# Part of the adaLN projection moved from TensorE to VectorE, and caches loaded earlier, in a two-layer diffusion backbone step

## Chip, cores and metric

One core of a Trainium2 chip runs the whole program in one launch. The metric is device time in microseconds (us). The kernel before took 1877.81 us as the median of three runs (1877.62, 1877.81 and 1882.55). A core has five engines that run their own instruction streams: PE (TensorE, matrix products), DVE (VectorE), ACT (ScalarE), POOL (GpSimd) and SP (SyncE, which here issues the DMAs). Each takes its instructions in program order and waits on semaphores for the others.

## The reference

Two layers work on 128 prompt tokens and 512 sample tokens of width 1024, in fp32. Each layer does, for either token group with its own conditioning vector:

```python
sh1, sc1, g1, sh2, sc2, g2 = split(silu(cond) @ ada_w[l] + ada_b[l], 6)   # adaLN, 1024 -> 6*1024
mix = mixers((x * (1 + sc1) + sh1) @ w_in[l])   # differential attention | neighbourhood attention | mLSTM
x = layer_norm(ALPHA * x + g1 * (mix @ w_out[l]))
y = square(relu((x * (1 + sc2) + sh2) @ w_mlp1[l])) @ w_mlp2[l]           # 1024 -> 4096 -> 1024
x = layer_norm(ALPHA * x + g2 * y)
```

There are two conditioning vectors (prompt and sample), so adaLN is a product of a 2 x 1024 matrix with a 1024 x 6144 matrix in each layer. The differential and the neighbourhood attention of the sample tokens also attend to 256 cached keys; the neighbourhood one adds a bias from a table per head.

## The kernel before

**Numbers.** Every fp32 matrix is split into a high and a low fp32r part; a product is three matmuls, high by high, high by low, low by high (`mul3`, L98 to L100), or two where one side is stacked (`mul2`, L106). A weight piece is split by ACT, which makes the high part (L170), and DVE, which subtracts it for the low part (L117).

**Weights.** All weights come as raw tiles of 1 MB. `run` walks a plan of units, finds the order in which the units first use each weight, and issues the loads in that order on SP (L208) into a ring of two buffers (`raw`). A buffer is free again when its four pieces are split into a slot, or, for an adaLN tile, when the unit that uses it is through. The slots are wt0 and wt1, and in the MLP a third one in the region AK. A scheduler then fixes each engine's instruction order, and this order is what runs.

**adaLN.** The 1024 x 6144 matrix of a layer is cut into 24 chunks of 1024 x 256, six vectors (shift, scale, gate, twice) of four chunks each, 48 in all. `ada_units` does a chunk with eight fp32 matmuls into four groups of 32 partitions (L368) and a copy by ACT (L371). A later "pick" adds the groups: with two small products into columns (L385) and a bias add on DVE (L388) for a shift or a scale, or, for a gate (vectors 2 and 5), with one product into a row of two partitions (L380), a bias row loaded from DRAM (L379) and a store of the gate row. In the plan, layer 0's vectors 0 and 1 come at the start, 2 to 4 are woven into its attention, vector 5 and layer 1's 0 and 1 stand in the first MLP, layer 1's 2 to 4 in its attention, and its vector 5 in the second MLP.

**MLP.** The hidden width 4096 is worked in eight rounds. The ups of a round are eight units of 24 matmuls with 128 hidden rows and 384 or 256 token columns; relu squared is made by ACT and DVE (L1389, L1390), and its split by ACT (L1401) and DVE (L117). The downs of the round before are five units, one for each tile of 128 tokens, of 24 matmuls with 512 columns into a PSUM tile `ss`, of which there are two. The first round's downs are copied to Y by ACT (L1414), the later ones added to Y by DVE (L1416). `downs[c - 1]` stands behind `ups[c]` in the plan, with spare adaLN units woven in.

**Neighbourhood attention.** `prep` loads the queries and keys of a head (hq, hk), then the head's cached keys into ckf, one buffer (L891), splits them into the last 256 columns of hk (ACT L892, DVE L893), and loads the bias table rw (L896), from which POOL makes three masked tables bm (L901). The scores of a head against its own and its cached keys are `mul2` products of hk with hq. In the differential attention the cached keys come through cak, one buffer (L1007).

Of the kernel before, what the change touches and what calls it, by code (L numbers as in the profile page):

```python
# [42 lines left out]
PACK = (("abT", (DEPTH, 48)), ("lnT", (DEPTH, 4, KT)), ("ident", (P,)), ("sel2", (2,)), ("selr", (32,)),  # L43
# [25 lines left out]
class Step:  # L69
# [61 lines left out]
    def w_src(self, k):  # L131
        kind, l, j = k
        d = self.d
        if kind == "ada":
            return d["ada"][l, j]
# [43 lines left out]
    def run(self, plan):  # L179
# [32 lines left out]
        def try_split(slack=0):  # L212
            while state["split"] < state["dma"] and order[state["split"]][0] == "ada":
                state["split"] += 1
# [23 lines left out]
        for i, u in enumerate(plan):  # L238
# [3 lines left out]
            for k in u.w:  # L242
# [6 lines left out]
                if k[0] != "ada":  # L249
# [12 lines left out]
            for k in u.w:  # L262
                if k[0] == "ada" and last[k] == i:
                    del self.raw[k]
# [21 lines left out]
    def setup(self):  # L286
# [30 lines left out]
        nc.vector.tensor_tensor(self.condS, self.condS, e, ALU.mult)  # L317

# [39 lines left out]
    def ada_units(self, l, vecs, own=None):  # L358
# [15 lines left out]
        def pick(v, q, part):  # L374
            po = self.mm("pick")
            if v in (2, 5):
                ab = self.adp.tile([2, CW], F32, name="abrow", bufs=1)
                off = v * D + q * CW
                nc.sync.dma_start(ab, self.d["ada_b"][l, off:off + CW].partition_broadcast(2))  # L379
                nc.tensor.matmul(po[:32, :CW], self.selr, part, start=True, stop=True)  # L380
                nc.vector.tensor_tensor(ab, po[:2, :CW], ab, ALU.add)
                nc.sync.dma_start(self.s_gate[l][v // 3][:, q * CW:(q + 1) * CW], ab)
            else:
                for b in range(2):
                    nc.tensor.matmul(po[:, 2 * b:2 * b + 2], part[:, b * P:(b + 1) * P], self.sel2,  # L385
                                     start=True, stop=True)
                c0 = v * KT + 2 * q
                nc.vector.tensor_tensor(  # L388
                    self.adaF[l][:, v, 2 * q:2 * q + 2, :], po[:, :4].rearrange("p (a b) -> p a b", b=2),
                    self.abT[:, l, c0:c0 + 2, None].to_broadcast([P, 2, 2]), ALU.add)  # L390
# [4 lines left out]
        return out  # L395

# [173 lines left out]
    def head_load(self, l, kind, h):  # L570
# [4 lines left out]
        k = self.hp.tile([P, NTOK + PAST], F32R, name="hk", tag="hk", bufs=2)  # L575
        for g in range(2):
            o = slice(64 * g, 64 * g + 64)
            nc.sync.dma_start(q[o].bitcast(F32), self.s_q[kind + "q"][l][f][rows])
            nc.sync.dma_start(k[o, :NTOK].bitcast(F32), self.s_q[kind + "k"][l][f][rows, g])
# [274 lines left out]
    def b_proj(self, l):  # L854
# [16 lines left out]
        return u  # L871

    def b_attn(self, l):
# [14 lines left out]
        def prep(h):  # L888
            q, k = self.head_load(l, "b", h)
            ck = self.bw.tile([P, PAST], F32, name="ckf", tag="ckf", bufs=1)  # L890
            nc.sync.dma_start(ck, d["cbk"][l, :, h])  # L891
            nc.scalar.activation(k[:, NTOK:], ck, AF.Copy, scale=0.125)  # L892
            nc.vector.scalar_tensor_tensor(k[64:, NTOK:], ck[64:], 0.125, k[64:, NTOK:].bitcast(F32),  # L893
                                           op0=ALU.mult, op1=ALU.subtract)
            rw = self.bw.tile([P, 8, 48], F32, name="rw", tag="rw", bufs=1)
            nc.sync.dma_start(rw, d["rpbw"][l, h])  # L896
            bm = []
            for v in range(3):
                b = self.bw.tile([P, 8, 32], F32, name="bm", tag="bm", bufs=4)
                o = 16 + BLK_OFF[v]  # L900
                nc.gpsimd.tensor_tensor(b, rw[:, :, o:o + 32], self.nmask[:, v, None, :].to_broadcast([P, 8, 32]), ALU.add)  # L901
                bm.append(b)
            hold[h] = (q, k, bm)
            hold[h, "r"] = self.bw.tile([P, 5], F32, name="br", tag="br", bufs=2)

        def scores(h, c):
# [9 lines left out]
            else:  # L916
# [3 lines left out]
                kl = k[:, P:NTOK].rearrange("p (r w) -> p r w", r=8)[:, :, w]  # L920
                self.mul2(ps[:, :256], kl, qq, stack_stationary=False)
                self.mul2(ps[:, 256:], k[:, NTOK:], qq, stack_stationary=False)
# [64 lines left out]
    def a_proj(self, l):  # L987
        nc, d = self.nc, self.d

        def op():  # L990
# [9 lines left out]
            nc.sync.dma_start(self.AV[:, 0:2], d["cav"][l])  # L1000

        held = {}

        def cached(g):
            if g < 4:
# [485 lines left out]
    def layer(self, l):  # L1491
# [75 lines left out]
        if more:  # L1567
            spare += self.ada_units(l + 1, (0, 1)) + [self.mod_unit(l + 1, 0)]
# [155 lines left out]
```

## Time and profile before

| | us |
|---|---|
| median of three runs | 1877.81 |
| the profiled execution | 1881.12 |
| its span, first to last instruction | 1879.3 |
| PE busy | 1790.4 (95%) |
| DVE busy | 1083.5 (58%) |
| ACT busy | 724.3 (39%) |
| first MLP's rounds | about 498 to 940 |
| layer 1's attention around the moved adaLN chunks | about 1095 to 1290 |

A profile is one execution. An engine's busy time is summed over its instructions, with overlaps counted once; matmul records overlap each other, since the next starts before the last has ended. A wait is read from the bracket of a row: the idle time before the instruction and what it ended with. [...]

### The profile page before, as it was taken

What the parts mean: (1) busy time and instruction counts of PE and PEld (TensorE: products, weight loads), DVE (VectorE), ACT (ScalarE), POOL (GpSimd) and SP (SyncE); (2) the same over time, 40 slices, a digit from 0 to 9 for tenths busy, and PEclk for the clock granted to TensorE, in tenths of its full rate; (3) what the DMA queues carried; (4) which work ended last, traced back from release to release, by engine and by line L of the source; (5) the groups of instructions that cost most, each with busy time, mean ns of one, the idle gap of its engine ahead of it and who ended that gap; (6) DMA issues with size and microseconds to landing.
All of it is one profiled execution on the core that took longest, in us unless ns stands there. A gap on an engine that the chain in (4) does not pass through costs nothing.

```text
span 1879.3 us, 29111 instructions
## 1 busy us (share of the span) xinstructions
PE 1790.4 (95%) x11666; PEld 1607.1 (86%) x11666; DVE 1083.5 (58%) x2068; ACT 724.3 (39%) x1640; POOL 100.4 (5%) x153
## 2 busy tenths in 40 slices
PE   6999999998999999999999989988989999999996
PEld 4999888887888888888899988877879889998895
DVE  4755566787623343345777645677977134544477
ACT  3343235456533231232364423353566223322220
POOL 1111100000000000000010210000010000000001
PEclk9999999999999999999999989989999999999998
DMA  9555465321423332333336655461214224222221
GB/s 352 163 165 163 164 201 189 111 85 57 146 68 102 123 115 91 109 107 140 106 116 222 162 167 179 145 214 64 85 45 146 90 90 157 69 90 68 75 94 56
DMA packets 82712, 239.23 MB, mean 127 GB/s; under 512 B 31808, under 2 KB 44544, under 8 KB 63888
## 3 DMA queue, kind: packets, MB, share of 16 engines
q1 hardware_dynamic: 82576, 237.36, 38.2%
q8 instruction: 92, 1.51, 0.3%
q14 instruction: 44, 0.36, 0.1%
HBM read 210.78 MB, written 26.55 MB: 126 GB/s over the span
## 4 chain that ended last, share of the span: by engine, by line
PE 82%; DVE 9%; DMA 5%; ACT 2%; issue 1%; SPq 1%; POOL 0%; DVEq 0%; ACTq 0%
PE m L98 15%; PE m L99 15%; PE m L100 15%; PE ss L98 7%; PE ss L99 7%; PE ss L100 7%; PE ss L1115 1%; PE m L1145 1%; PE m L961 1%; PE m L368 1%; DVE wt L117 1%; DMA ada<-ada 1%; DVE anm L1118 1%; DMA z<-s_x 1%; PE mz L106 1%
## 5 line engine op out<-in xcount | busy, mean ns | idle before, releaser
L98 PE MATMUL m<-wt,Th 128*128 128x256 f32 (+2 forms) x864 | 274.8, 319 | 7.1 <-DVE Tl L1206 2.8
L99 PE MATMUL m<-wt,Th 128*128 128x256 f32 (+2 forms) x864 | 269.1, 312 | 0.0
L100 PE MATMUL m<-wt,Tl 128*128 128x256 f32 (+2 forms) x864 | 267.0, 311 | 0.0
L98 PE MATMUL m<-Th,AK 128*128 128x384 f32 (+1 forms) x736 | 229.3, 312 | 4.9 <-DVE Th L112 4.2
L99 PE MATMUL m<-Tl,AK 128*128 128x384 f32 (+1 forms) x736 | 229.1, 312 | 0.9 <-DVE Tl L117 0.9
L100 PE MATMUL m<-Th,AK 128*128 128x384 f32 (+1 forms) x736 | 225.9, 311 | 0.0
L170 ACT ACTIVATE wt<-raw 128x512 fp32r<-128x512 f32 x244 | 146.7, 627 | 149.3 <-PE ss L100 85.6
L117 DVE TENSOR_TENSOR wt<-raw,wt 128x512 fp32r<-128x512 f32 x244 | 162.3, 693 | 47.1 <-ACT wt L170 46.2
L98 PEld LDWEIGHTS m<-wt,Th 128*128 128x128 f32 x864 | 168.6, 195 | 22.4 <-issue 5.5
L100 PEld LDWEIGHTS m<-wt,Tl 128*128 128x128 f32 x864 | 167.4, 195 | 10.8 <-issue 3.1
L99 PEld LDWEIGHTS m<-wt,Th 128*128 128x128 f32 x864 | 169.0, 196 | 7.6 <-issue 1.7
L98 PE MATMUL m<-Th,wt 128*128 128x384 f32 (+1 forms) x536 | 166.4, 311 | 0.0
L100 PE MATMUL m<-Th,wt 128*128 128x384 f32 (+1 forms) x536 | 166.2, 310 | 0.0
L99 PE MATMUL m<-Tl,wt 128*128 128x384 f32 (+1 forms) x536 | 165.9, 310 | 0.0
L1416 DVE TENSOR_TENSOR Y<-ss,Y 128x1024 f32<-128x1024 f32 x60 | 73.2, 1223 | 156.8 <-PE ss L100 156.8
L1390 DVE SCALAR_TENSOR_TENSOR rl<-m,rl 128x384 f32<-128x384 f32 (+1 forms) x128 | 62.2, 488 | 164.5 <-ACT rl L1389 164.5
L98 PEld LDWEIGHTS m<-Th,AK 128*128 128x128 f32 x736 | 140.7, 191 | 8.8 <-DVE Th L112 4.7
L99 PEld LDWEIGHTS m<-Tl,AK 128*128 128x128 f32 x736 | 140.7, 191 | 3.7 <-issue 1.6
L100 PEld LDWEIGHTS m<-Th,AK 128*128 128x128 f32 x736 | 140.5, 191 | 1.0 <-issue 0.8
L98 PE MATMUL ss<-wt,hid 128*128 128x512 f32 x356 | 139.7, 395 | 0.0
L1389 ACT ACTIVATE rl<-m 128x384 f32<-128x384 f32 (+1 forms) x128 | 55.3, 434 | 218.8 <-PE m L100 216.1
L99 PE MATMUL ss<-wt,hid 128*128 128x512 f32 x356 | 138.8, 391 | 0.0
(705 smaller groups left out, 3554.4 us busy)
## 6 DMA issues: line engine op xcount, KB each, us to landing
raw<-w SPq DMA_DIRECT2D x64, 1024.0 KB
raw<-ada SPq DMA_DIRECT2D x40, 1024.0 KB
raw<-w_in SPq DMA_DIRECT2D x24, 1024.0 KB
ada<-ada SPq DMA_DIRECT2D x8, 1024.0 KB
raw<-w_out SPq DMA_DIRECT2D x8, 1024.0 KB
s_x<-Y SPq DMA_DIRECT2D x15, 512.0 KB
hq<-s_cq SPq DMA_DIRECT2D x16, 320.0 KB
nb<-s_nm SPq DMA_DIRECT2D x16, 320.0 KB
```

The source lines that it names most:

```text
L98: mt(out, a[0], b[0], start=first, stop=False)
L99: mt(out, a[0], b[1], start=False, stop=False)
L100: mt(out, a[1], b[0], start=False, stop=last)
L106: self.nc.tensor.matmul(out, a, b, start=first and i == 0, stop=last and i == 1)
L117: self.nc.vector.tensor_tensor(out, x, hi.bitcast(F32), ALU.subtract)
L170: self.nc.scalar.activation(hi, r, AF.Copy)
L368: nc.tensor.matmul(ps[32 * g:32 * g + 32, :CW], self.condS[:, kt, :], raw[:, kt, :], start=kt % 2 == 0, stop=kt % 2 == 1)
L961: nc.tensor.matmul(out[64 * i:64 * i + 64], w, rhs, start=b == 0, stop=b == nb - 1)
L1115: nc.tensor.matmul(ps[:, b, :384], qq[i], K[:, j, b * 384:b * 384 + 384], start=i == 0, stop=i == 1)
L1389: nc.scalar.activation(r[:, :n], ps[:, :n], AF.Relu)
L1390: nc.vector.scalar_tensor_tensor(r[:, :n], ps[:, :n], 0.0, r[:, :n], op0=ALU.max, op1=ALU.mult)
L1416: nc.vector.tensor_tensor(y, ps, y, ALU.add)
```

## The change

Of the 48 adaLN chunks 20 stay on TensorE: layer 0's vectors 0 to 4. The other 28 (layer 0's vector 5 and all of layer 1's) are done on VectorE in the first MLP. Their weights arrive transposed (`adaT`: 256 output rows of 1024 inputs in a 1 MB tile, two rows for each partition), and both conditioning vectors stand broadcast on all partitions (`condB`). A chunk is four multiply-and-sum operations over 128 x 1024, two output rows by two vectors; each sum lands in the column of `adaF` where it belongs. The bias add follows once for a vector. Gates are now kept as columns like the others, and `gate_rows` turns them into DRAM rows with two transposes, a copy and a DMA. In the plan one such chunk stands behind each down until there are none left: 5, 5, 4, 5, 5 and 4 in rounds 1 to 6, the unit that uses layer 1's first two vectors having one of the places.

The second part is the neighbourhood attention: the cached keys of all heads are loaded and split once a layer, before the projections of its queries, into a tile `BK` of their own; the first two bias tables are loaded there too, with two buffers, and the masked tables get six. The third is the cached keys of the differential attention: two buffers, and the first two loads are issued where the tiles are made.

```diff
+    def ada_dve(self, l, vecs):
+        nc = self.nc
+        def emit(v, q):
+            raw = self.raw[("adt", l, 4 * v + q)].rearrange("p (a b) -> p a b", b=D)
+            for b in range(2):
+                for j in range(2):
+                    x = self.mw.tile([P, D], F32, name="adx", tag="z2", bufs=2)
+                    nc.vector.scalar_tensor_tensor(x, raw[:, b], 1.0, self.condB[:, j], op0=ALU.mult, op1=ALU.mult,
+                                                   accum_out=self.adaF[l][:, v, 2 * q + b, j:j + 1])
+            if q == 3:
+                a = self.adaF[l][:, v]
+                nc.vector.tensor_tensor(a, a, self.abT[:, l, KT * v:KT * v + KT, None].to_broadcast([P, KT, 2]), ALU.add)
+                if v in (2, 5):
+                    self.gate_rows(l, v)
+        return [Unit(0, lambda v=v, q=q: emit(v, q), (("adt", l, 4 * v + q),), soft=True) for v in vecs for q in range(4)]
+    def gate_rows(self, l, v):
+        def rows():
+            pt = self.mm("pick")
+            for j in range(2):
+                nc.tensor.transpose(pt[:KT, j * P:j * P + P], self.adaF[l][:, v, :, j], self.ident)
+            row = self.adp.tile([KT, 2, P], F32, name="grow", tag="adpart", bufs=2)
+            nc.scalar.activation(row, pt[:KT, :2 * P].rearrange("k (j p) -> k j p", j=2), AF.Copy)
+            nc.sync.dma_start(self.s_gate[l][v // 3].rearrange("j (k p) -> k j p", p=P), row)
+        self.defer(rows)
...
# in setup: silu of both conditioning vectors, to DRAM for the broadcast
+        nc.sync.dma_start(r, d["condr"])
+        nc.scalar.activation(e, r, AF.Exp, scale=-1.0)
...
+        nc.sync.dma_start(self.s_cond.rearrange("j (a b) -> (j a) b", b=2 * D // P), r)
...
# neighbourhood attention
-        k = self.hp.tile([P, NTOK + PAST], F32R, name="hk", tag="hk", bufs=2)
+        k = self.hp.tile([P, NTOK], F32R, name="hk", tag="hk", bufs=2)
+        def cached():
+            ck = self.hp.tile([P, H, PAST], F32, name="ckf", tag="ckf", bufs=1)
+            nc.sync.dma_start(ck, d["cbk"][l])
+            k = self.BK = self.hp.tile([P, H, PAST], F32R, name="BK", tag="BK", bufs=1)
+            nc.scalar.activation(k, ck, AF.Copy, scale=0.125)
+            nc.vector.scalar_tensor_tensor(k[64:], ck[64:], 0.125, k[64:].bitcast(F32), op0=ALU.mult, op1=ALU.subtract)
+            self.rw = {}
+            for h in range(2):
+                self.rpb(l, h)
-        u = self.proj_fm(l, 4, self.sink_fm(l, "bq"))
+        u = [Unit(0, cached, soft=True)] + self.proj_fm(l, 4, self.sink_fm(l, "bq"))
...
-                b = self.bw.tile([P, 8, 32], F32, name="bm", tag="bm", bufs=4)
+                b = self.bw.tile([P, 8, 32], F32, name="bm", tag="bm", bufs=6)
-                self.mul2(ps[:, 256:], k[:, NTOK:], qq, stack_stationary=False)
+                self.mul2(ps[:, 256:], self.BK[:, h], qq, stack_stationary=False)
...
# differential attention
+            held[g] = self.at.tile([P, 2, PAST], F32, name="cak", tag="cak", bufs=2)
...
# the plan
-        ada = self.ada_units(l, (2, 3, 4))
+        ada = self.ada_units(l, (2, 3, 4) if l == 0 else ())
-        spare = self.ada_units(l, (5,))
+        spare = []
         if more:
-            spare += self.ada_units(l + 1, (0, 1)) + [self.mod_unit(l + 1, 0)]
+            spare = self.ada_dve(l, (5,)) + self.ada_dve(l + 1, (0, 1)) + [self.mod_unit(l + 1, 0)]
+            spare += self.ada_dve(l + 1, range(2, 6))
         for c in range(1, NFF - 1):
             P_ += ups[c]
-            P_ += weave(downs[c - 1], spare[:2] if c < NFF - 2 else spare)
-            spare = spare[2:]
+            for x in downs[c - 1]:
+                P_ += [x] + spare[:1]
+                spare = spare[1:]
```

In the changed kernel's own numbering the accumulating operation is L426, the vector's bias add L430, the Y add L1476 (L1416 before), relu squared L1450 (L1390 before) and the raw loads L210 (L208 before).

On VectorE, in the downs of the first MLP, the queue before was this (ss is a down's PSUM tile, AK the low pieces of the next w1 tile, hid the low half of relu squared, adaF the picked adaLN columns):

```order
L1390 SCALAR_TENSOR_TENSOR rl_6623<-m3_6598,rl_6623 128x256
L117 TENSOR_TENSOR hid1_5236<-rl_6623,hid1_5236 128x256
L1416 TENSOR_TENSOR Y_99<-ss_6640,Y_99 128x1024
L1416 TENSOR_TENSOR Y_99<-ss_6666,Y_99 128x1024
L388 TENSOR_TENSOR adaF1_88<-m3_6757,pack_75 128x4
L1416 TENSOR_TENSOR Y_99<-ss_6705,Y_99 128x1024
L1416 TENSOR_TENSOR Y_99<-ss_6731,Y_99 128x1024
L117 TENSOR_TENSOR AK_1981<-raw_6703,AK_1981 128x512 x2
L1416 TENSOR_TENSOR Y_99<-ss_6761,Y_99 128x1024
L117 TENSOR_TENSOR AK_1981<-raw_6703,AK_1981 128x512
L388 TENSOR_TENSOR adaF1_88<-m2_6870,pack_75 128x4
L117 TENSOR_TENSOR AK_1981<-raw_6703,AK_1981 128x512
```

and now, in round 2 of the same MLP (adx is the scratch that the accumulating operation writes, raw_6244, raw_6280 and raw_6317 are adaT tiles, raw_6353 is the next w1 tile):

```order
L1476 TENSOR_TENSOR Y_110<-ss_6282,Y_110 128x1024
L430 TENSOR_TENSOR adaF1_99<-adaF1_99,pack_75 128x16
L426 SCALAR_TENSOR_TENSOR adx_6347,adaF1_99<-raw_6280,condB_5242 128x1024
L426 SCALAR_TENSOR_TENSOR adx_6349,adaF1_99<-raw_6280,condB_5242 128x1024
L426 SCALAR_TENSOR_TENSOR adx_6351,adaF1_99<-raw_6280,condB_5242 128x1024
L426 SCALAR_TENSOR_TENSOR adx_6381,adaF1_99<-raw_6317,condB_5242 128x1024
L1476 TENSOR_TENSOR Y_110<-ss_6319,Y_110 128x1024
L426 SCALAR_TENSOR_TENSOR adx_6383,adaF1_99<-raw_6317,condB_5242 128x1024
L426 SCALAR_TENSOR_TENSOR adx_6385,adaF1_99<-raw_6317,condB_5242 128x1024
L426 SCALAR_TENSOR_TENSOR adx_6387,adaF1_99<-raw_6317,condB_5242 128x1024
L1476 TENSOR_TENSOR Y_110<-ss_6355,Y_110 128x1024
L117 TENSOR_TENSOR AK_1999<-raw_6353,AK_1999 128x512 x4
```

Three or four accumulating operations now stand between two Y adds, and the first low piece of the next w1 tile stands behind all of them. Before, two pieces stood ahead of the last Y add.

On SP, the raw loads around the same place were, before (ada is an adaLN tile, w1 and w2 the MLP's):

```order
L208 DMA raw_6628<-ada 128x2048
L208 DMA raw_6638<-ada 128x2048
L208 DMA raw_6703<-w1 128x2048
L208 DMA raw_6800<-w1 128x2048
L208 DMA raw_6808<-w2 128x2048
L208 DMA raw_6942<-w2 128x2048
L208 DMA raw_7072<-ada 128x2048
L208 DMA raw_7082<-ada 128x2048
```

and are now:

```order
L210 DMA raw_6068<-w2 128x2048
L210 DMA raw_6198<-adaT 128x2048
L210 DMA raw_6208<-adaT 128x2048
L210 DMA raw_6244<-adaT 128x2048
L210 DMA raw_6280<-adaT 128x2048
L210 DMA raw_6317<-adaT 128x2048
L210 DMA raw_6353<-w1 128x2048
L210 DMA raw_6389<-w1 128x2048
L210 DMA raw_6399<-w2 128x2048
```

Five adaT tiles stand between the w2 tiles of one round and the w1 tiles of the next, where two ada tiles stood before, in the same ring of two buffers.

On PE, at the start of layer 1's neighbourhood attention, the scores of the first two heads (my and mz) stood in this order before; the second pair of products is the one with the cached keys (the second piece is 49 rows later in the queue):

```order
L100 MATMUL m1_10649<-wt1_101,Tl_98 128x256
L106 MATMUL my_10746<-hk_10574,hq_10573 128x256 x2
L106 MATMUL mz_10758<-hk_10728,hq_10727 128x256 x2
L368 MATMUL mw_10853<-raw_10323,condS_73 32x256 x8
L98 MATMUL m2_10675<-wt1_101,Th_97 128x256
```

```order
L99 MATMUL m3_10701<-wt1_101,Th_97 128x256
L100 MATMUL m3_10701<-wt1_101,Tl_98 128x256
L106 MATMUL my_10746<-hk_10574,hq_10573 128x256 x2
L98 MATMUL m1_10770<-wt0_100,Th_97 128x256
L99 MATMUL m1_10770<-wt0_100,Th_97 128x256
```

and now:

```order
L99 MATMUL m1_10750<-wt1_112,Th_108 128x256
L100 MATMUL m1_10750<-wt1_112,Tl_109 128x256
L106 MATMUL my_10847<-hk_10679,hq_10678 128x256 x2
L106 MATMUL my_10847<-BK_9771,hq_10678 128x256 x2
L106 MATMUL mz_10861<-hk_10831,hq_10830 128x256 x2
L106 MATMUL mz_10861<-BK_9771,hq_10830 128x256 x2
L98 MATMUL m2_10776<-wt1_112,Th_108 128x256
```

The products with cached keys now follow directly on those with the head's own, and take them from BK, and the adaLN matmuls (L368) are gone from there.

## Rows read from the trace of the kernel before

**Rows 1.** Page, busy time of each engine (share of the span) and instructions.

```profile
PE 1790.4 (95%) x11666; PEld 1607.1 (86%) x11666; DVE 1083.5 (58%) x2068; ACT 724.3 (39%) x1640; POOL 100.4 (5%) x153
```

**Rows 2.** Page, chain that ended last: shares of the span by engine.

```profile
PE 82%; DVE 9%; DMA 5%; ACT 2%; issue 1%; SPq 1%; POOL 0%; DVEq 0%; ACTq 0%
```

**Rows 3.** Windows: stretch, length, busy PE, PEld, DVE, ACT, POOL, PEclk, DMA share, GB/s.

```profile
498.00:940.00 442.00, 442.00 (x2578) 390.25 (x2578) 201.33 (x322) 133.51 (x263) 2.38 (x4) 1.00 0.32 109
605.00:665.00 60.00, 60.00 (x354) 50.73 (x354) 23.55 (x39) 17.41 (x35) 0.00 (x0) 1.00 0.34 110
1095.00:1290.00 195.00, 175.74 (x1404) 153.60 (x1403) 119.15 (x276) 74.22 (x189) 11.38 (x17) 0.94 0.53 170
```

**Rows 4.** Windows, adaLN matmuls of L368 alone: length, busy PE, PEld, PEclk.

```profile
540.00:640.00 100.00, 5.17 (x64) 2.31 (x64) 1.00 0.28 95
640.00:880.00 240.00, 12.22 (x128) 4.97 (x128) 1.00 0.35 119
1095.00:1290.00 195.00, 14.13 (x192) 6.15 (x192) 0.94 0.53 170
1470.00:1580.00 110.00, 5.17 (x64) 2.31 (x64) 1.00 0.31 107
```

**Rows 5.** Windows, picks alone: L385 of eight chunks, then L380 of four.

```profile
640.00:880.00 240.00, 4.11 (x32) 5.02 (x32) 1.00 0.35 119
...
540.00:640.00 100.00, 2.48 (x8) 0.55 (x8) 1.00 0.28 95
```

**Rows 6.** Timeline of PE, a chunk and a pick, each with the next matmul.

```profile
566.02 1.09 PE L368 MATMUL m<-raw,condS 128*32 128x256 f32 x16
...
567.04 0.45 PE L100 MATMUL m<-Th,AK 128*128 128x384 f32 x1
...
739.70 0.50 PE L385 MATMUL m<-pack,adpart 128*128 128x2 f32 x4
...
740.06 0.49 PE L98 MATMUL ss<-wt,hid 128*128 128x512 f32 x1
```

**Rows 7.** Timeline, cached neighbourhood keys: start, duration, instruction, idle before.

```profile
189.05 0.80 PE L106 MATMUL my<-hk,hq 128*128 128x256 f32 x2 [3.75 <-DVE hk L893]
...
1101.69 0.40 PE L106 MATMUL mz<-hk,hq 128*128 128x256 f32 x2
...
1108.96 0.50 SPq L891 DMA_DIRECT2D ckf<-cbk  x1
...
1117.45 0.79 PE L106 MATMUL mz<-hk,hq 128*128 128x256 f32 x2 [6.87 <-DVE hk L893]
```

**Rows 8.** Windows, the stretches around these two waits.

```profile
187.80:194.60 6.80, 5.55 (x26) 5.55 (x27) 4.75 (x10) 1.89 (x5) 2.57 (x3) 0.50 0.36 116
1112.80:1123.00 10.20, 5.55 (x26) 5.55 (x27) 5.36 (x11) 3.73 (x8) 2.13 (x3) 0.50 0.58 190
```

**Rows 9.** Groups by form, VectorE: busy us, mean ns of one, idle before.

```profile
L117 DVE TENSOR_TENSOR AK<-raw,AK 128x512 fp32r<-128x512 f32 x148 | 97.8, 687 | 60.9 <-ACT AK L170 60.3
L1416 DVE TENSOR_TENSOR Y<-ss,Y 128x1024 f32<-128x1024 f32 x60 | 73.2, 1223 | 156.8 <-PE ss L100 156.8
L926 DVE RECIPROCAL br<-br 128x1 f32<-128x1 f32 x40 | 6.4, 161 | 13.7 <-ACT bp L925 13.5
L1436 DVE SCALAR_TENSOR_TENSOR x<-Y,mv,lnrows 128x1024 f32<-128x1024 f32 x4 | 5.1, 1277 | 0.0
L388 DVE TENSOR_TENSOR adaF<-m,pack 128x4 f32<-128x4 f32 x16 | 2.5, 155 | 11.2 <-PE m L385 11.2
```

**Rows 10.** Timeline of PE, second MLP: a down's first matmul, and the next unit's.

```profile
1613.87 0.39 PE L98 MATMUL ss<-wt,hid 128*128 128x512 f32 x1
...
1619.33 0.33 PE L100 MATMUL m<-Th,wt 128*128 128x384 f32 x1
```

**Rows 11.** Timeline, second MLP: a raw load's issue, and the split that waited.

```profile
1621.99 0.33 SPq L208 DMA_DIRECT2D raw<-w  x1
...
1627.14 0.63 ACT L170 ACTIVATE wt<-raw 128x512 fp32r<-128x512 f32 x1 [0.58 <-DMA raw<-w]
```

More of the change, by code (lines that the diff above doesn't have):

```diff
@@ L134, in w_src @@
         if kind == "ada":
-            return d["ada"][l, j]
+            return d["ada"][j]
+        if kind == "adt":
+            return d["adaT"][j + (4 if l else -20)]
         if kind == "in":
@@ L212, in try_split @@
         def try_split(slack=0):
-            while state["split"] < state["dma"] and order[state["split"]][0] == "ada":
+            while state["split"] < state["dma"] and order[state["split"]][0] in ("ada", "adt"):
                 state["split"] += 1
@@ L262, in run @@
             for k in u.w:
-                if k[0] == "ada" and last[k] == i:
+                if k[0] in ("ada", "adt") and last[k] == i:
                     del self.raw[k]
@@ L375, in pick @@
             po = self.mm("pick")
[L376 to L390, printed above, removed]
+            for b in range(2):
+                nc.tensor.matmul(po[:, 2 * b:2 * b + 2], part[:, b * P:(b + 1) * P], self.sel2,
+                                 start=True, stop=True)
+            c0 = v * KT + 2 * q
+            nc.vector.tensor_tensor(
+                self.adaF[l][:, v, 2 * q:2 * q + 2, :], po[:, :4].rearrange("p (a b) -> p a b", b=2),
+                self.abT[:, l, c0:c0 + 2, None].to_broadcast([P, 2, 2]), ALU.add)
+            if v == 2 and q == 3:
+                self.gate_rows(l, v)
         for v in vecs:
@@ L889, in prep @@
             q, k = self.head_load(l, "b", h)
[L890 to L896, printed above, removed]
+            rw = self.rw[h]
             bm = []
             for v in range(3):
-                b = self.bw.tile([P, 8, 32], F32, name="bm", tag="bm", bufs=4)
+                b = self.bw.tile([P, 8, 32], F32, name="bm", tag="bm", bufs=6)
                 o = 16 + BLK_OFF[v]
@@ L1000, in op, with load @@
             nc.sync.dma_start(self.AV[:, 0:2], d["cav"][l])
+            for g in range(2):
+                load(g)
         held = {}
+        def load(g):
+            held[g] = self.at.tile([P, 2, PAST], F32, name="cak", tag="cak", bufs=2)
+            nc.sync.dma_start(held[g], d["cak"][l, :, 2 * g:2 * g + 2])
         def cached(g):
-            if g < 4:
-                held[g] = self.at.tile([P, 2, PAST], F32, name="cak", tag="cak", bufs=1)
-                nc.sync.dma_start(held[g], d["cak"][l, :, 2 * g:2 * g + 2])
             if g:
```

41 lines of the change are left out of this document (31 added, 10 removed).

## The prediction

> **What bounds the kernel now.** I read the busy shares first. TensorE is busy for 1790.4 of 1879.3 us, VectorE for 1083.5 [rows 1]. The chain of waits agrees: 82% of the path is PE, 9% DVE, 5% DMA [rows 2]. So whatever leaves TensorE shortens the run, unless something else is late. The busy table by stage says how much room there is. In the first MLP (498 to 940 us) PE is busy for all of 442.00 us at full clock, and DVE for 201.33; in one round of it, 605 to 665 us, DVE has 23.55 of 60. In the second layer's attention (1095 to 1290 us) PE is busy for 175.74 of 195, so 19.3 us are waits [rows 3]. Two views are left: what the adaLN matmuls cost, and which waits the early loads take away.
>
> The profiled execution took 1881.1 us around its span; the median of the runs is 1877.8, 3.3 less. I add up against 1881.1 and take 3.3 off at the end.
>
> **What leaves TensorE.** 28 chunks lose their 8 matmuls and their pick: 12 in the first MLP, 12 in layer 1's attention, 4 in layer 1's MLP. The eight matmul records (16, as fp32 is two passes) of the moved chunks sum to 5.17 + 12.22 in the first MLP, 14.13 in the attention and 5.17 in the second MLP [rows 4]. Picks add 4.11 for eight chunks into columns and 2.48 for four into gate rows [rows 5]; the attention has both kinds (6.5), the second MLP the gate kind. By busy rows that is 24.0, 20.6 and 7.7, 52.3 us. A busy row overstates, since the next matmul starts before the last is through: the chunk at 566.02 lets the next matmul start at 567.04, 1.02 us later; the pick at 739.70 lets it start at 740.06, 0.36 later [rows 6]. These give 28 × 1.38 = 38.6, the low end. The mean busy chunk is 36.7 / 28 = 1.31; taking the lapped 0.29 (1.31 − 1.02) off each of 28 gives 44.2 (20.5, 17.2 and 6.5), which is what I use, since it keeps the picks' larger mean. In the attention some of the 17.2 now fills waits of other work, which stay. With 19.3 us idle there and DVE busy for 119 of 195 us, I count 14. **Gain 41.0**, ends 30.3 (the 38.6 with half of the attention's twelve, 8.3, lost to waits) and 49.1 (52.3 less 3.2).
>
> **What the early loads remove.** PE waits 6.87 us at 1117.45 and 3.75 at 189.05 for the split cached key, L893; in layer 1 the load was issued only at 1108.96, because ckf has one buffer [rows 7]. After the change all four heads' keys are split during the projection, tens of microseconds ahead of use. Next in line are the head's own keys and queries, with which mz already ran at 1101.69, so the wait should go whole: 10.6 us. [...] **Gain 16.2**. The low end is 8, one of the two turned into a wait for something else. The second cak buffer has nothing behind it on the path; I cost it at nothing, under projection matmuls. Without that cover it would cost one load.
>
> **What is added outside the MLP.** Four gate stages with two transposes each, against picks of the same kind that are gone: 1.4 us by the 0.36 of a pick for four pairs. At the start two more DMA issues on SP ahead of the first weights, 0.33 each like the one at 1621.99 [rows 11], and two small DVE operations like L388, 0.155 each [rows 9]: 1.0. **Cost 2.4**, ends 0 and 5.
>
> **What VectorE gets.** Each chunk is four scalar_tensor_tensor over 128x1024 with an accumulated sum. The trace has none. The nearest row, L1436, is the same operation on the same tile without the sum: 1277 ns; writing a 128x1 result by itself costs 161 (L926) [rows 9]. So a is between 1.28 and 1.44 us, by these rows, or twice that if the sum needs a second pass (a rival). 112 of them are 143 to 161 us on an engine that is busy for 201 of 442. On average they fit: a round has five downs of 5.46 us (1613.87 to 1619.33 [rows 10]) and as many columns in its ups, 54.6 us; DVE has 39% of that, 21.4, plus 20 × 1.28 to 1.44, 26 to 29, so 47 to 50 of 54.6.
>
> They are not spread evenly, though. They stand behind the downs, in an order that is fixed on an in-order engine. Take a round with five chunks, as in the order of round 2, and count from the end of its second down. PE goes on with three downs, 16.4, and six matmuls of the next ups that need only the high half, 0.9. Before that the third down waits 1.1 for a free PSUM tile: two tiles, and the Y add takes 1.22 [rows 9]. Together 18.4. DVE in the same time has five Y adds (6.1), the bias add (0.2), twelve accumulating operations (15.4 to 17.3) and only then the first low piece of the next w1 tile (0.69), 22.4 to 24.3. PE needs that piece: a **stall of 4.0 to 5.9**, I take 4.9. A stall like this brings the half clock, as in rows 8, for 2.8. Rounds 2, 4 and 5 have this pattern: 3 × 7.7 = 23.1. The first round writes Y on ScalarE and has no Y adds in that queue. Rounds 3 and 6 have four chunks, four operations less: 5.1 to 5.8 less, no stall or a small one, 1 us each. The 1.1 of PSUM comes in five rounds, 5.5. **Cost 30.6**; the low end is 12 (stalls of 4.0 without the half clock), the high end 39 (5.9 each, and the half clock in rounds 3 and 6 too).
>
> One more thing is moved: the w1 tile for the next round is loaded only when a raw buffer is free, and the last five adaT tiles stand before it on SP. It is released by the fourth chunk, four accumulating operations and two Y adds (7.6 us) before DVE reaches its first piece. A load and the high piece take 5.15 from issue to ScalarE's start (1621.99 to 1627.14 [rows 11]) plus 0.63, so the load is hidden, with about 1.8 to spare.
>
> **Sum.** −41.0 − 16.2 + 2.4 + 30.6 = −24.2; 1881.1 − 24.2 − 3.3 = **1854**. Its own range: with chunks at 49.1 and the stage's cost at 18, between the low end and mine, 1833; with chunks at 30.3 and its high end, 1873.
>
> **Rivals.** First, VectorE hides everything: no stall in the MLP. For it: the average load is at most 92%, and ups are woven with downs, so the low pieces could come earlier. Against it: the order has five downs' queue before the piece. 1881.1 − 54.8 − 3.3 = 1823 (54.8 is the sum without the stage's 30.6); with the busy sum of chunks 1815.
>
> Second, the raw ring is the bound. If landings take longer than 5.15, with 28 adaLN tiles in this stage instead of 12 (it moved 109 GB/s before [rows 3]), PE waits for a whole landing each round: 5.15 + 0.63 + 2.8 of half clock = 8.6, six times, 51.5, plus the 5.5 for PSUM. 1881.1 − 54.8 + 57.0 − 3.3 = 1880, no change. Against it: the DMA share was 0.32 there.
>
> Third, slower: the accumulating operation makes a second pass over its 1024 columns. Then a is 2 × 1.277 + 0.161 = 2.71, and a round of DVE is 21.4 + 4.67 × 4 × 2.71 = 72.0 against PE's 54.6: 17.4 in each of six rounds, 104.6. 1881.1 − 54.8 + 104.6 − 3.3 = **1928**. It decides from a = 1.78 on, where 21.4 + 18.67a reaches 54.6. For it: no row of this kernel shows an operation with accum_out on DVE. Against it: on ScalarE the sum of an activation is a short operation behind it, not a second pass, and L1436 with two fp32 inputs takes 1277 ns where the two-input add L1416 takes 1223 [rows 9]; the two inputs alone halve nothing.
> [...]
> [...]
>
> **Chances.** Forecast 0.60, all hidden 0.15, the ring 0.12, second pass 0.10, anything else 0.03. The difference that a measurement here can tell is about 0.3%, 5.6 us. The forecast's range ends about where that bound lies, 1872, so faster is 0.58 + 0.15 + 0.02; the ring case gives most of the unchanged 0.10, the second pass and part of the ring case the slower 0.15. The range runs from 1820, just under the all-hidden case, to 1882, just over the ring case; it leaves out the second pass, the busy-sum end of the first rival, and the 0.03.
>
> **What would show it.** In the changed profile: PE busy for some 60 us less (the chunks' busy rows and the two half clocks); no PE wait for a cached key near 189 and 1117; the accumulating lines at 1.28 to 1.44 us in mean; in rounds 2, 4 and 5 of the first MLP a PE wait of about 5 us for the first low piece of w1 at the end of the downs, at half clock behind it; the third down behind a Y add by about 1 us. The stall would be wrong if PE's first-MLP stretch has no idle time; the ring rival is right if the wait ends on ScalarE's high piece and that on the raw DMA; the second pass if the lines show 2.5 us or more.

## The result, and the profile after

| | before | after |
|---|---|---|
| median of the runs, us | 1879.9 | 1845.8 |
| profiled execution, us | 1881.1 | 1844.9 |
| its span, us | 1879.3 | 1843.0 |

The ratio is 0.9815 (95% interval 0.9801 to 0.9830): 34 us faster, where 24 were forecast. The forecast of 1854 us was 8 too high; 1845.8 lies in the range. (The median before is 1879.9 here, with a fourth run; the forecast started from the 1877.8 of three.)

The page of the changed kernel, busy shares and chain of waits, against [rows 1, 2]:

```profile
PE 1746.1 (95%) x11146; PEld 1582.6 (86%) x11146; DVE 1199.2 (65%) x2268; ACT 711.9 (39%) x1611; POOL 101.3 (5%) x153
...
PE 77%; DVE 13%; DMA 5%; ACT 3%; issue 1%; SPq 1%; POOL 0%; DVEq 0%; ACTq 0%; POOLq 0%
PE m L98 15%; PE m L100 15%; PE m L99 15%; PE ss L98 6%; PE ss L99 6%; PE ss L100 6%; DVE adx L426 2%; PE ss L1171 1%; PE m L1012 1%; PE m L1201 1%; DVE wt L117 1%; DVE AK L117 1%; DVE anm L1174 1%; PE mz L106 1%; DMA cak<-cak 1%
...
L426 DVE SCALAR_TENSOR_TENSOR adx<-raw,condB 128x1024 f32<-128x1024 f32 x112 | 131.9, 1219 | 21.2 <-DMA raw<-adaT 21.1
```

PE lost 44.3 us of busy time, where the prediction named some 60 as a sign; by an estimate from their rows (below), about 5 of the difference are two stretches at a reduced clock (0.69 and 0.60) behind new waits; the rest stays open. DVE gained 115.7 and is now on the chain with the accumulating operations; it waited 21.1 us itself for adaT tiles to land. The windows of [rows 3], now (PEclk is the TensorE clock that was granted, as a share of the full one):

```profile
498.00:940.00 442.00, 433.93 (x2404) 388.36 (x2403) 332.61 (x558) 135.54 (x269) 3.04 (x6) 1.00 0.44 152
605.00:665.00 60.00, 58.00 (x318) 51.79 (x319) 47.83 (x86) 15.46 (x32) 0.00 (x0) 1.00 0.47 166
1095.00:1290.00 195.00, 175.44 (x1267) 159.14 (x1266) 135.71 (x294) 81.70 (x204) 6.65 (x10) 0.93 0.34 100
```

Around round 2 of the first MLP DVE is busy for 47.8 of 60 us. That is 80%, under the forecast 47 to 50 of 54.6 (86 to 92%). PE now has some idle time (58.00 of the 60 us are busy), at a granted clock of 1.00 throughout. What PE waits for in the first MLP, in total, times, longest:

```profile
PE ss L98 <- DVE Y L1476: 5.2, 5, 1.4
PE m L100 <- DVE AK L117: 1.9, 3, 0.8
PE ss L99 <- DVE AK L117: 0.4, 1, 0.4
PE m L98 <- ACT AK L172: 0.3, 1, 0.3
```

The waits are those that were named: five times the third down behind a Y add, and the low piece of w1 at the end of the downs. The first has the forecast size (5.5). The second comes in rounds 2, 4 and 5, as named, but with 0.76, 0.57 and 0.54 us in place of 4.9.

Where the time went, by start times of the same matmuls in the two profiled executions: the first up of the first MLP, its last down, the first down of the second MLP, and the end.

| stage | before | after | measured | forecast |
|---|---|---|---|---|
| to the first MLP | 494.5 | 494.8 | +0.3 | −5.2 |
| first MLP | 456.8 | 446.8 | −10.0 | +11.2 |
| layer 1's attention | 487.3 | 467.0 | −20.3 | −23.7 |
| second MLP and end | 440.7 | 434.5 | −6.3 | −6.5 |

The forecast column is the sum's terms by stage (the first MLP: −20.5, +30.6 and three of the four gate stages, 0.36 each). Nearly the whole error, 21 us, is the first MLP; 5.5 and 3.4 the other way stand in the two attention stages.

### The profile page after: what moved, and what is told of

It reads as the page before. It is cut to its first block, busy times and chain, and to the rows that moved or that the text cites. A ratio compares the mean times of both kernels' runs of the same rounds, so it can differ in the third digit from the quotient of the medians.

```text
span 1843.0 us, 28181 instructions
## 1 busy us (share of the span) xinstructions
PE 1746.1 (95%) x11146; PEld 1582.6 (86%) x11146; DVE 1199.2 (65%) x2268; ACT 711.9 (39%) x1611; POOL 101.3 (5%) x153
## 3 DMA queue, kind: packets, MB, share of 16 engines
q8 instruction: 88, 1.44, 0.3%
## 4 chain that ended last, share of the span: by engine, by line
PE 77%; DVE 13%; DMA 5%; ACT 3%; issue 1%; SPq 1%; POOL 0%; DVEq 0%; ACTq 0%; POOLq 0%
PE m L98 15%; PE m L100 15%; PE m L99 15%; PE ss L98 6%; PE ss L99 6%; PE ss L100 6%; DVE adx L426 2%; PE ss L1171 1%; PE m L1012 1%; PE m L1201 1%; DVE wt L117 1%; DVE AK L117 1%; DVE anm L1174 1%; PE mz L106 1%; DMA cak<-cak 1%
## 5 line engine op out<-in xcount | busy, mean ns | idle before, releaser
L117 DVE TENSOR_TENSOR wt<-raw,wt 128x512 fp32r<-128x512 f32 x252 | 167.3, 692 | 75.5 <-ACT wt L172 74.3
L98 PE MATMUL m<-Th,AK 128*128 128x384 f32 (+1 forms) x672 | 209.5, 313 | 4.7 <-DVE Th L112 4.2
L99 PE MATMUL m<-Tl,AK 128*128 128x256 f32 (+1 forms) x672 | 209.5, 312 | 0.4 <-DVE Tl L117 0.3
L100 PE MATMUL m<-Th,AK 128*128 128x256 f32 (+1 forms) x672 | 207.7, 312 | 1.9 <-DVE AK L117 1.9
L98 PE MATMUL m<-Th,wt 128*128 128x256 f32 (+1 forms) x600 | 185.9, 310 | 0.0
L99 PE MATMUL m<-Tl,wt 128*128 128x256 f32 (+1 forms) x600 | 185.7, 310 | 0.0
L100 PE MATMUL m<-Th,wt 128*128 128x256 f32 (+1 forms) x600 | 185.3, 310 | 0.0
L98 PE MATMUL ss<-wt,hid 128*128 128x512 f32 x356 | 140.8, 396 | 5.2 <-DVE Y L1476 5.2
L426 DVE SCALAR_TENSOR_TENSOR adx<-raw,condB 128x1024 f32<-128x1024 f32 x112 | 131.9, 1219 | 21.2 <-DMA raw<-adaT 21.1
L100 PE MATMUL ss<-wt,hid 128*128 128x512 f32 x356 | 140.5, 395 | 0.0
L99 PE MATMUL ss<-wt,hid 128*128 128x512 f32 x356 | 140.3, 394 | 0.0
L172 ACT ACTIVATE AK<-raw 128x512 fp32r<-128x512 f32 x140 | 85.6, 628 | 133.7 <-PE ss L100 69.1
L1476 DVE TENSOR_TENSOR Y<-ss,Y 128x1024 f32<-128x1024 f32 x60 | 73.2, 1222 | 94.8 <-PE ss L100 94.8
L1450 DVE SCALAR_TENSOR_TENSOR rl<-m,rl 128x384 f32<-128x384 f32 (+1 forms) x128 | 62.2, 488 | 110.2 <-ACT rl L1449 109.9
L98 PEld LDWEIGHTS m<-Th,AK 128*128 128x128 f32 x672 | 127.3, 190 | 7.1 <-DVE Th L112 4.6
```

The costliest lines, as they stand in the source:

```text
L98: mt(out, a[0], b[0], start=first, stop=False)
L99: mt(out, a[0], b[1], start=False, stop=False)
L100: mt(out, a[1], b[0], start=False, stop=last)
L117: self.nc.vector.tensor_tensor(out, x, hi.bitcast(F32), ALU.subtract)
L172: self.nc.scalar.activation(hi, r, AF.Copy)
L426: nc.vector.scalar_tensor_tensor(x, raw[:, b], 1.0, self.condB[:, j], op0=ALU.mult, op1=ALU.mult, accum_out=self.adaF[l][:, v, 2 * q + b, ...
```

## The experiments

Each ran beside the kernel before on the same chip. Times are medians; the changed kernel is 1845.8 in its first runs.

**Which part brings what.** Four kernels: the changed one without the third part, without the second and third, and the kernel before with the early loads alone, with and without the third part.

```diff
# cak_back: the changed kernel; each load again where cached(g) had it
-            for g in range(2):
-                load(g)
-... name="cak", tag="cak", bufs=2)
+... name="cak", tag="cak", bufs=1)
# adaln_only: also hk of NTOK + PAST columns, ckf and rw loaded in prep, bm of 4 buffers, as before
# early_only: the kernel before with BK, rw, bm and cak of the change; early_nocak: without cak
```

> The changed kernel with the third part undone: one cak buffer, each load issued where it was before. Theory A: the two new waits of PE in the neighbourhood attention come from the cak part. In layer 0 PE waits 5.85 us at 207.75 for a softmax on ScalarE that stands behind a split of cak, which itself had waited 7.10 us for its load; in layer 1 it waits 5.68 us at 1100.80 for queries whose load was issued at 1088.38, beside two cak loads issued at 1091.71. Without the early loads both waits go, with the 2 to 3 us that each cost in granted clock behind it (0.69 in 207.9 to 215, 0.67 in 1100 to 1110): 1845.8 less 8 to 17, that is 1829 to 1838. Theory B: PE only comes to these places earlier, since the adaLN chunks that stood there are gone, and waits for whatever is next; then the time stays within 4 us of 1845.8, and the waits are there under other names.

Measured: 1846.6 (ratio to before 0.981 to 0.985). Theory A fell: the waits of 5.5 and 5.7 us are there without the early cak loads.

> The changed kernel with its second and third part undone, so that only the move of 28 adaLN chunks to VectorE is left. By the prediction's terms the cached-key waits come back and cost 16.2: 1862. By theory A (the cak part took with one hand what the keys gave with the other) the keys' waits of 3.75 and 6.87 come back, and the 5.85 and 5.68 go: 1845.8 within 4 us, 1842 to 1850.

Measured: 1858.1. Neither: the early loads are worth 12.3 us on top of the move, between the 16.2 and nothing. The move alone is worth 22.0, the 1880.1 of before less this.

> The kernel before with the second and third part alone: all 48 chunks stay on TensorE, keys, tables and cak load early. By the prediction's term: 1879.9 less 16.2, 1864. By theory A the cak loads put waits of their own in the same places, as in the changed kernel: 1875 to 1883. If it is under 1868, the new waits belong to the missing adaLN matmuls and theory B has it.

Measured: 1871.0, between the theories.

> The kernel before with the second part alone (keys and bias tables early, bm with six buffers), cak as before. By the prediction's term and by theory A alike: the waits of 3.75 and 6.87 us and the half clock behind them go, 1879.9 less 10 to 16.2, 1864 to 1870. By theory B PE waits for the next thing in the same place, and it stays above 1875.

Measured: 1869.9, 10.2 less than before: the low part of the range of theory A and the prediction. With early_only at 1871.0, the third part gives nothing, as it was costed. The profile of early_nocak says how the 10.2 come about; PE's waits around the two places of [rows 7] (150 to 240 and 1030 to 1130 us):

```profile
PE my L368 <- ACT bp L937: 5.0, 1, 5.0
...
PE my L106 <- ACT bp L937: 1.2, 1, 1.2
```

In layer 1 the 6.87 became 1.2. In layer 0 the 3.75 became 5.0: PE comes to the next adaLN chunk sooner, and waits there for the PSUM tile of a softmax. That softmax stands behind a split of cak, on ScalarE itself and, with the mask add and the maximum ahead of it, on VectorE. In the changed kernel:

```profile
196.60 0.41 SPq L1059 DMA_DIRECT2D cak<-cak  x1
...
203.32 0.63 ACT L1064 ACTIVATE AK<-cak 128x512 fp32r<-128x512 f32 x1 [7.10 <-DMA cak<-cak]
...
203.98 1.33 DVE L117 TENSOR_TENSOR AK<-cak,AK 64x512 fp32r<-64x512 f32 x2 [6.59 <-ACT AK L1064]
205.34 0.43 DVE L974 TENSOR_TENSOR my<-my,bm 128x256 f32<-128x256 f32 x1
...
206.14 0.69 DVE L975 TENSOR_REDUCE bnm<-my 128x1 f32<-128x512 f32 x1
...
206.92 0.69 ACT L976 ACTIVATE bp<-my,bnm 128x512 f32<-128x512 f32 x1 [2.06 <-DVE bnm L975]
...
207.75 0.68 PE L380 MATMUL my<-raw,condS 128*32 128x256 f32 x4 [5.85 <-ACT bp L976]
```

The third cak load is issued at 196.60, when a buffer of the two is free, and ScalarE waits 7.10 us for it, with the softmax (L976) behind it in the queue. VectorE waits 6.59 us for ScalarE's high part, with the mask add (L974) and the maximum (L975) of the softmax behind the low part. With one buffer (cak_back) it is the first loads that come late, and the wait is about as long (5.5). In layer 1 of the changed kernel, where the adaLN chunks are gone too, another load is next:

```profile
1088.38 0.48 SPq L617 DMA_DIRECT2D hq<-s_bq  x1
...
1100.80 0.55 PE L106 MATMUL mz<-hk,hq 128*128 128x256 f32 x1 [5.68 <-DMA hq<-s_bq]
```

In the kernel before, the same load was issued only a little later, and PE used the queries at 1101.69 [rows 7]:

```profile
1090.56 0.44 SPq L578 DMA_DIRECT2D hq<-s_bq  x1
```

In early_nocak, with the chunks in place, the same product ran without a wait:

```profile
1099.86 0.40 PE L106 MATMUL mz<-hk,hq 128*128 128x256 f32 x2
```

Without the chunks PE is through with the products of my, and waits, from 1095.1 on. The changed kernel has one more such wait, which the kernel before has not:

```profile
1045.58 0.30 PE L98 MATMUL m<-Cst,hq 128*128 128x130 f32 x1 [2.28 <-DMA hq<-s_cq]
```

**Taking the two waits away.** cak4 has four cak buffers, hq3 three buffers for queries.

```diff
# cak4
-            for g in range(2):
+            for g in range(4):
                 load(g)
-... name="cak", tag="cak", bufs=2)
+... name="cak", tag="cak", bufs=4)
-                if g < 3:
-                    load(g + 1)
# hq3
-... name="hq", tag="hq", bufs=2)
+... name="hq", tag="hq", bufs=3)
```

> The changed kernel with four cak buffers instead of two, all four loads issued where the first two are. The wait of 5.85 us at 207.75 in layer 0 stands behind the third and fourth split of cak, which wait for a load issued at 196.60 that lands at 203.32. Theory A: with the loads issued some 10 us sooner that wait goes, with the half clock behind it: 1845.8 less 4 to 8, unless layer 1's queries come later by the two loads more that run beside them, which costs up to 3. Theory B: PE waits there for the second pair of heads in any case; within 2 of 1845.8.

Measured: 1841.7, 4.1 less: theory A at its low end, but with four runs from 1839.8 to 1847.8 not clear of noise. The trace is clearer. The wait of layer 0 is gone, and the first up of the first MLP starts at 487.4 instead of 494.8. In layer 1 PE waits 6.2 us at the old place, and the attention takes 475.8 instead of 467.0 (473.4 in the changed kernel's repeat below).

> The changed kernel with three hq buffers instead of two. In layer 1 PE waits 5.68 us at 1100.80 for the second head's queries, whose load is issued at 1088.38, when a buffer comes free behind the recurrent heads. Theory A: with a third buffer the load is issued earlier (its source is stored long before) and the wait goes, with the 2 to 3 us of half clock: 1845.8 less 6 to 9. Theory B: the load waits for the DMA queues, which are 0.94 busy from 1090 to 1100, and PE for the next thing: within 2 of 1845.8.

Measured: 1837.8, 8.0 less; theory A. The load is issued at 1080.01 and PE no longer waits for it; the next wait there is 2.0, for a softmax. The 2.28 at the earlier load of queries is gone too, so the 8.0 are not the one wait alone.

**What the accumulating operations cost.** short_ops cuts each to 64 columns, double issues each twice.

```diff
# short_ops
-nc.vector.scalar_tensor_tensor(x, raw[:, b], 1.0, self.condB[:, j], ...
+nc.vector.scalar_tensor_tensor(x[:, :64], raw[:, b, :64], 1.0, self.condB[:, j, :64], ...
# double: a loop around the same operation
+                    for _ in range(2):
...
```

> The changed kernel with the 112 accumulating operations cut from 1024 to 64 columns (the sums are then over 64 columns; loads, order and everything else as they are). Theory A: in the first MLP the 5.2 us of waits for a Y add come from the pair of interleaved downs whose PSUM tiles come free one Y add later, with no adaLN matmuls in between any more to fill PE, and only the 1.9 us of waits for the low piece come from the accumulating operations: 1845.8 less 1 to 3. Theory B: both kinds of wait come from VectorE being full: less 6 to 8, 1838 to 1840. By the prediction's sizes of this stage (30.6 us of cost) it would be less 25.

Measured: 1851.9, slower by 6, which no theory had. In the stage itself theory A holds in kind: the waits for the low piece are gone and those for a Y add stay. They are longer than before, though:

```profile
PE ss L98 <- DVE Y L1476: 9.4, 5, 3.4
```

From the first up to the last down the first MLP takes 445.8 against 446.8. Most of the 6 lies in layer 1's attention (471 against 467), where the profile of the changed kernel's repeat has 473 itself; why the median is higher stays open. What is shown is that cutting 94% of the columns gives the first MLP no more than 1 us back: the 2.6 us of waits for pieces go, and those for a Y add grow by 4.2. The Y add waits do not come from the accumulating operations.

> The changed kernel with every accumulating operation issued twice. It measures what one more operation costs a VectorE that is nearly full. Back to back these operations start 1.146 us apart in the changed kernel, though the rows say 1.22 and 0.08. Theory A, the price is the distance of the starts: a round with five chunks has 40 x 1.146 = 46 us of them beside some 20 of other work, 66 against PE's 57, and one with four has 57: four rounds 9 longer, 1880 at least, up to 1900 if the low pieces behind the downs wait for more than the mean. Theory B, the price is the sum of the durations, 1.30: 52 + 21 = 73 and 63 against 57, 16 and 6 longer, 1922 at least.

Measured: 1957.8, 112 more than the changed kernel, and above both theories' figures (up to 1900; 1922 at least). The time does not confirm theory B: back to back the operations start 1.146 us apart in this profile too. Both theories thought of VectorE's queue alone, and the profile shows another mechanism:

```profile
641.71 0.33 SPq L210 DMA_DIRECT2D raw<-w  x1
...
646.68 1.67 ACT L172 ACTIVATE AK<-raw 128x512 fp32r<-128x512 f32 x3 [39.34 <-DMA raw<-w]
...
647.36 0.69 PE L98 MATMUL m<-Th,AK 128*128 128x384 f32 x1 [16.08 <-ACT AK L172]
```

and behind it the clock:

```profile
647.00:655.00 8.00, 7.64 (x30) 7.57 (x31) 6.26 (x12) 1.87 (x4) 0.00 (x0) 0.59 0.23 69
```

The w1 tile is loaded only when VectorE has let go of a raw buffer, and lands 5.0 us later; PE waits 16.08 us for the high piece, and four more waits of this kind in the stage are 9.2 to 18.5. The first MLP is 110 us longer than in the changed kernel. This is the raw ring, the second rival, in a kernel in which VectorE is too late. So in this run the price of a late VectorE is not the lateness of its queue alone: in these five places a landing (5.0 us at the 16.08) and a split (0.7 from ScalarE's start to PE's) come on top, and behind the 16.08 a stretch at a mean clock of 0.59.

**Where the chunks stand.**

```diff
# spread: the five chunks of a round behind other units
+            five = spare[:5]
+            spare = spare[5:]
+            for i, x in enumerate(ups[c] + downs[c - 1]):
+                P_ += [x] + (five[:1] if i in (1, 3, 5, 7, 8) else [])
+                five = five[1:] if i in (1, 3, 5, 7, 8) else five
```

> The changed kernel with the chunks of a round behind the second, fourth, sixth and eighth up and the first down, instead of one behind each of the five downs. Theory A: the queue of accumulating operations behind the downs is what makes PE wait for the low piece (1.9 us in all); spread out, these waits go, and the five of 1.0 us for a Y add stay: less 1 to 3. Theory B: the order of the raw ring matters more. adaT tiles then stand between the w1 and w2 tiles, a weight's load waits until VectorE has worked off the chunk ahead of it, and PE waits for weights: 5 or more slower than the changed kernel.

Measured: 1845.9, as the changed kernel. The rounds gained and the start lost: PE's waits for a Y add are gone, first up to last down take 442.3 instead of 446.8. This is theory A the wrong way round, since the waits for the low piece stay (three, 2.5 in all). But at the first ups PE now waits 4.83 for the high half of its input and 2.31 for the low one, where it waited 2.12 before and after. On VectorE the first chunk has come to stand ahead of that half, and waits for the broadcast vectors:

```profile
494.07 1.23 DVE L426 SCALAR_TENSOR_TENSOR adx<-raw,condB 128x1024 f32<-128x1024 f32 x1 [2.88 <-DMA condB<-s_cond]
...
495.22 0.42 DVE L112 CAST Th<-pf 128x512 fp32r<-128x512 f32 x1
```

No theory had this wait at the start.

**The start, a repeat, and a faster version.** late_cond makes the second copy of the conditioning vectors after the first weights' loads (its load is issued at 33.58 instead of 1.17 us). best has that, hq with three buffers in layer 1, and cak with four in layer 0.

```diff
# late_cond: condr, its silu and s_cond move from setup into
+    def cond_rows(self):
# best, beside it
+            for g in range(2 if l else 4):
+... name="cak", tag="cak", bufs=2 if l else 4)
+... name="hq", tag="hq", bufs=3 if l else 2)
```

> The changed kernel itself once more, as the yardstick for the three runs beside it, which differ from it by a few us. All theories: 1842 to 1849.

Measured: 1847.4 (1845.2 to 1851.5). Its profiled execution was 6.7 us longer in span than the first one, 6.4 of it in layer 1's attention; so differences of some us in one profile's attention stage are not a finding.

> The changed kernel with the second copy of the conditioning vectors (load, silu, store for the broadcast) made after the first weights instead of ahead of them. The first projection matmul at full length starts at 43.62 in the changed kernel and at 40.85 before. Theory A: the two DMA issues and four small operations ahead of the first weights make the 2.8 us; without them 1845.8 less 1.5 to 3. Theory B: the start is bound by the landing of the weights and varies by itself from run to run (42.1 to 43.9 in the kernels run so far that carry it); within 1 of the changed kernel.

Measured: 1851.1, 3.6 more than the repeat beside it, with runs that overlap (1848.8 to 1855.8). Theory A fell: the first full projection starts at 43.28, as before the edit.

> The changed kernel with three edits that the runs so far point to: four cak buffers in layer 0 with all loads issued at once (two in layer 1), three hq buffers in layer 1 (two in layer 0), and the second copy of the conditioning vectors made later. If the waits are independent, the gains add: 4.1 and 8.0 by the single runs, and up to 3 from the start, 1830 to 1834. If they are one wait that moves on, the sum is no better than the larger, 1838.

Measured: 1830.3, ratio to before 0.9726 (0.9708 to 0.9744), and 17 less than the changed kernel beside it. The gains add, and the waits are independent. That it is more than the 12.1 of the single runs is not traced to the end; two things in the profiles go with it. In cak4 the four buffers lost time in layer 1, where this kernel has two. And the start is earlier than in any other changed kernel: of the 10.5 us by which the first MLP begins sooner, 4.1 are there at the first full projection (39.56 against 43.62; 42.1 to 43.9 in the others). In its profile the two waits are gone; what is left around them is one of 2.0 us in layer 1:

```profile
PE my L106 <- ACT bp L978: 2.0, 1, 2.0
```

## Why the prediction came out as it did

The direction and the mechanism were right: work left TensorE, VectorE had room for it, and in the first MLP the new waits are those that were named. The range held. That the time came within 8 us is in part luck: the stage's cost was set 22.8 too high, and the gains and the start were missed by some 11 the other way. Its steps:

**The stall behind the downs was mis-sized.** The step said: VectorE needs 22.4 to 24.3 us from the end of the second down to the first low piece, PE 18.4, so a stall of 4.9, half clock behind it, three times. In round 2 VectorE runs:

```profile
603.95 1.23 DVE L1476 TENSOR_TENSOR Y<-ss,Y 128x1024 f32<-128x1024 f32 x1 [1.74 <-PE ss L100]
605.09 1.22 DVE L426 SCALAR_TENSOR_TENSOR adx<-raw,condB 128x1024 f32<-128x1024 f32 x1
...
614.31 0.08 DVE L426 DVE_READ_ACCUMULATOR adx<-raw,condB 128x1 f32 x1
614.31 1.22 DVE L426 SCALAR_TENSOR_TENSOR adx<-raw,condB 128x1024 f32<-128x1024 f32 x1
615.45 0.08 DVE L426 DVE_READ_ACCUMULATOR adx<-raw,condB 128x1 f32 x1
615.45 1.22 DVE L426 SCALAR_TENSOR_TENSOR adx<-raw,condB 128x1024 f32<-128x1024 f32 x1
...
623.45 2.49 DVE L117 TENSOR_TENSOR AK<-raw,AK 128x512 fp32r<-128x512 f32 x4
```

From the first Y add to the low piece it takes 19.5, 20.2 with the piece. The rows have 1.22 and 0.08 us for an accumulating operation, 1.30 together, inside the bounds of 1.28 to 1.44. But the next one starts 1.14 to 1.15 after it: the rows overlap. Five Y adds and twelve accumulating operations at their distances are 5 × 1.14 + 12 × 1.146 + 0.1 = 19.5. I had added durations. For TensorE I had used the distance of the starts, and the same could be read for VectorE in the trace of before, where a 0.68 operation is followed 0.59 later:

```profile
1290.63 0.68 DVE L1285 SCALAR_TENSOR_TENSOR Y<-z,Y 128x512 f32<-128x512 f32 x1
1291.22 0.95 DVE L1118 TENSOR_REDUCE anm<-ss 128x1 f32<-128x768 f32 x1
```

PE took somewhat more than the forecast, with the third down at 605.23 and the six matmuls at the end, and waited 0.76:

```profile
605.23 0.50 PE L98 MATMUL ss<-wt,hid 128*128 128x512 f32 x1 [0.86 <-DVE Y L1476]
...
623.15 0.28 PE L99 MATMUL m<-Tl,AK 128*128 128x256 f32 x1
624.19 0.44 PE L100 MATMUL m<-Th,AK 128*128 128x384 f32 x1 [0.76 <-DVE AK L117]
```

So the forecast 30.6 is 7.8 in the trace, below its own low end of 12 (which left the 5.5 for the Y adds out): 5.2 of 5.5 for the Y adds, 2.6 for pieces instead of 14.7 and 2.0, and nothing of the 8.4 of half clock, as the stage's clock is 1.00. That the half clock follows a short stall was carried over from waits of 3.75 and 6.87 us, and the 2.8 for each was an estimate that no run shows (below).

**The chunks' price.** The first MLP shortened by 10.0 with 7.8 of new waits and three gate stages, 1.1 by the prediction's price, so 18.9 of chunks left TensorE there, where 20.5 were counted; the second MLP gave 4.8 between its first and last down in every run of the changed form, where 6.5 were counted. Together these are 1.48 us for each of 16 chunks, between the low bound of 1.38 and the 1.58 that was used. In layer 1's attention the move alone gave 13.3 in one profile (474.0 in adaln_only against 487.3), where 14 were counted; the repeat shows that this stage differs by up to 6.4 between executions.

**The early loads** gave 12.3 of the 16.2, and 10.2 without the move. The 16.2 are 10.6 of waits and 2.8 of half clock behind each. The 2.8, half of the 5.55 us busy there [rows 8], was an estimate, and no run shows it; the stall behind the downs and the ring rival were added up with it too. What the trace of before shows is how far apart these matmuls start, 0.213 us at a granted clock of 0.50 and 0.12 at 1.00, with the window of the second stretch:

```profile
193.49 0.41 PE L98 MATMUL m<-wt,Th 128*128 128x256 f32 x1
193.70 0.41 PE L99 MATMUL m<-wt,Th 128*128 128x256 f32 x1
193.91 0.41 PE L100 MATMUL m<-wt,Tl 128*128 128x256 f32 x1
...
196.87 0.28 PE L98 MATMUL m<-wt,Th 128*128 128x256 f32 x1
196.99 0.28 PE L99 MATMUL m<-wt,Th 128*128 128x256 f32 x1
197.11 0.28 PE L100 MATMUL m<-wt,Tl 128*128 128x256 f32 x1
```

```profile
194.60:200.00 5.40, 5.40 (x47) 5.40 (x47) 0.85 (x2) 0.00 (x0) 0.00 (x0) 1.00 0.78 225
```

By an estimate from these rows the 26 matmuls of the first stretch would have taken 26 × (0.213 − 0.12) = 2.4 us less. In layer 0 a wait came back at the next place, the softmax behind a cak split (above): of the 6.6 counted there, early_nocak and early_only came to the first MLP 3.3 and 0.5 us sooner. In layer 1 the early loads without the move took 9.6 and 11.1 off the attention, where 9.7 were counted. With the move, the step "Next in line are the head's own keys and queries, with which mz already ran at 1101.69" failed there: the queries were in time because PE still had the adaLN chunks to work on. The granted clock behind the two new waits shows that they cost more than their length:

```profile
207.90:215.00 7.10, 7.10 (x52) 5.88 (x50) 2.17 (x7) 2.30 (x6) 0.00 (x0) 0.69 0.44 148
1101.00:1108.00 7.00, 7.00 (x39) 7.00 (x40) 3.25 (x8) 2.29 (x6) 0.65 (x1) 0.60 0.43 137
```

**The start** was forecast at 1.0 and was 2.8 in the first profile (43.62 against 40.85 for the first full projection). late_cond does not take it away, and best, with the same edit, starts at 39.56; its cause stays open.

**The rivals.** All hidden (1823) comes nearest in mechanism, since the 2.6 us of waits for pieces are all that VectorE's load costs; but the waits for a Y add came, and the gains were smaller than it assumed. The second pass is refuted: the operation with its sum starts every 1.146 us, the plain add on a tile of the same size every 1.14. Its sum is a row of 0.08 us behind it, as the sum on ScalarE, which the prediction set against this rival, is one of 0.19 in the trace of before:

```profile
1120.32 0.69 ACT L925 ACTIVATE bp<-my,bnm 128x512 f32<-128x512 f32 x1 [2.00 <-DVE bnm L924]
1120.91 0.19 ACT L925 ACTIVATION_READ_ACCUMULATOR bp<-my,bnm 128x1 f32 x1
```

The ring did not bind PE here (0.3 us of one wait ended on ScalarE's high piece), and does with twice the work.

## What to carry to other kernels

Price an operation in a queue by the distance between starts; here that held on TensorE (in the trace of before matmuls of 512 columns start 0.23 us apart, with rows of 0.39) and on VectorE (1.146 us, with rows of 1.22 and 0.08). The duration of a row counted only at the end of the queue, where the last piece's row made 20.2 us of 19.5. Before a wait is counted as gone, look for what is next in the same engine's queue and in the DMA queue, and ask whether it was on time only because of the wait; here each of two removed waits left another of 5 to 6 us (in layer 1 only together with the move), and buffers for those, with the edit of the start beside them, gave 17 us more, of which some 4 at the start are not explained. Look also at which engine holds the buffers of a load ring: where VectorE held them and was late (double), PE paid a landing of 5.0 us on top of that lateness.

## What was not expected of the hardware

An accumulating operation over 128x1024 fp32 has two rows, 1219 and 82 ns on average of 112, and takes 1.146 us in a queue, within 0.01 us of an add without a sum. Waits of TensorE of up to 1.4 us in the first MLP left the granted clock at 1.00; the two of 5.7 and 5.9 us were followed by stretches at 0.60 and 0.69.
